# FFN1's down product by seven half-size products, and the modulation's rows made in three other places

## The chip, the cores and the metric

The kernel runs on one NeuronCore of a Trainium2 chip. The metric is the device time of one execution in microseconds, the median of several runs. Engines are called by their names: TensorE (PE), VectorE (DVE), ScalarE (ACT), GpSimd (POOL) and SyncE (SP), which issues nearly all transfers here.

## What is computed

One decoder layer in float32 on 1024 tokens of width 1024: a half step of a gated feed-forward network (FFN1), a mixer of two attention branches, and another half step (FFN2). Each is wrapped in norms, and nine rows of 1024 numbers, made from a conditioning vector c, shift, scale and gate them. Cut to what matters here:

```python
def swiglu(h, w_gate, w_up, w_down):
    return (jax.nn.silu(h @ w_gate) * (h @ w_up)) @ w_down          # 1024 -> 2816 -> 1024

mod = (jax.nn.silu(c) @ w_mod[l] + b_mod[l]).reshape(B, N_MOD, D_MODEL)
sh1, sc1, gt1, sh2, sc2, gt2, sh3, sc3, gt3 = [mod[:, j, None, :] for j in range(N_MOD)]
h = rms_norm(x, g_pre_ffn1[l]) * (1 + sc1) + sh1
x = x + 0.5 * gt1 * rms_norm(swiglu(h, w_gate1[l], w_up1[l], w_down1[l]), g_post_ffn1[l])
u = rms_norm(x, g_pre_mix[l]) * (1 + sc2) + sh2
y = hybrid_mixer(u, ...)      # branch A: sparse attention; branch B: three groups of dilated attention
x = x + gt2 * rms_norm(y, g_post_mix[l])
h = rms_norm(x, g_pre_ffn2[l]) * (1 + sc3) + sh3
x = x + 0.5 * gt3 * rms_norm(swiglu(h, w_gate2[l], w_up2[l], w_down2[l]), g_post_ffn2[l])
```

## The kernel before

Each matrix product in float32 is made of three matmuls on a high and a low part of both operands (`mm3`, lines 104 to 106); `split` (L76 on ACT, L77 on VectorE) makes the parts. The program is written stage by stage; a scheduler then puts each engine's instructions into one fixed order, and each engine works through its list in that order. A transfer is an entry of SP's list: while it waits for its buffer, all later transfers wait behind it.

The stages, in order of time:

- FFN1's gate and up (`gate_up`, 25 to 500 us): products by a scheme of seven half-size products instead of eight, 11 blocks `b` of 256 columns. The activations go to DRAM (`act1`).
- FFN1's down (`down`, 500 to 757 us): 22 slices of 128 rows of the weights by 8 token tiles and two halves of the columns, plainly, 352 matmuls on each line of `mm3`.
- The mixer: its first products (`cpj`), the indexer's scores, the top-k selection on VectorE (`topk`, 1035 to 1281 us) with the gates' products under it, branch B (`branch_b`: three groups of eight tiles, T0 to T23; tile T ends with the sum `ob`, L1064, and its store `bd<-ob`, L1069), branch A (`branch_a`, from 1445 us: keys `kpj` from the latents `gbuf`, scores `as`, and so on), and the output projection `wo`.
- FFN2: gate and up by `gate_up`, and down by `down7`, which is a scheme of seven half-size products as well, 308 matmuls on each line. It reads eight prepared operands per block from DRAM, which FFN2's `gate_up` writes with one more addition and two subtractions on POOL and one subtraction on VectorE (`operands`, lines 298 to 325, the subtractions on L302).

Rows 2 to 8 of the modulation come from `mod_rest`, a generator: one step loads a 128x512 piece of w_mod (`wr`, 256 KB), and VectorE multiplies it by a column of silu(c) and adds it to a sum (`macc`, L185; the first of eight by L183). After eight steps the sum over the partitions is made by two matmuls with a matrix of ones (`mo`), and half a row is stored. FFN1's gate_up and down call it as a filler, two steps at a time, in four buffers:

```python
r = pool.tile([P, 512], F32, name="wr", tag="wr", bufs=4)
nc.sync.dma_start(r, i["w_mod"][0, k * P:(k + 1) * P, c0:c0 + 512])
```

In `wo`, most norms (`residual`, `prenorm` and within them `rsqrt`, lines 84 to 100) are on POOL. Branch A's queries (`queries`, L1158) read 512-byte pieces from DRAM.

Of the kernel before, what the change touches and what calls it, by code (L numbers as in the profile page):

```python
# [10 lines left out]
F32 = mybir.dt.float32  # L11
# [12 lines left out]
P = 128  # L24
# [4 lines left out]
LATE = 2  # L29
FILL = 2  # L30
# [9 lines left out]
class Layer:  # L40
# [125 lines left out]
    def mod_rest(self, pool, rows):  # L166
# [3 lines left out]
        for v in (2, 3, 4, 5, 6, 7, 8):  # L170
            for h in range(2):
                c0 = v * D + h * 512
                acc = pool.tile([P, 512], F32, name="macc")
                for k in range(8):
                    r = pool.tile([P, 512], F32, name="wr", tag="wr", bufs=4)
# [12 lines left out]
                ah = pool.tile([P, 512], F32R, name="mah", tag="wr", bufs=4)  # L188
                al = pool.tile([P, 512], F32R, name="mal", tag="wr", bufs=4)
# [62 lines left out]
    def gate_up(self, W, raws, pools, V, wg, wu, actd=None, ad=None):  # L252
# [93 lines left out]
        def steps(order, filler=None, ahead=()):  # L346
# [4 lines left out]
            for s, (b, i) in enumerate(order):  # L351
# [4 lines left out]
                for m in range(2):  # L356
# [19 lines left out]
                    if i in (1, 4, 5, 6):  # L376
                        if m == 0:
                            nc.scalar.activation(x[0], x[0], AF.Silu)  # L378
                        else:
                            nc.gpsimd.tensor_tensor(x[1], x[1], x[0], op=ALU.mult)  # L380
                            if ad is not None:
                                operands(b, i, x)
                                continue
                            ff, h = {1: (0, 0), 4: (1, 0), 5: (1, 1), 6: (0, 1)}[i]
                            nc.sync.dma_start(actd[2 * b + ff, :, h * 512:(h + 1) * 512], x[1])
                if filler is not None and b >= len(early):
                    for _ in range(FILL):
                        next(filler, None)
# [11 lines left out]
    def down(self, W, wd, room, actd, y, G, junk, ss, post, filler=None):  # L400

        nc = self.nc
        NF = DFF // P
        tags = ("tr", "tr", "o", "gg", "pj", "pj", "s", "pt")
        got = [0]
        bg = iter(())
        for dh, tiles in ((0, range(8)), (1, range(4)), (1, range(4, 8))):
            bk = {t: self.bank("dn", tag=tags[t]) for t in tiles}
            halves = sorted({t // 4 for t in tiles})
            late, last = [], dh == 1  # L410
            nlate = LATE if dh and tiles[-1] == 7 else 1

            def mul(t, c, w, a):
                ts = slice((t % 4) * P, (t % 4 + 1) * P)
                ah, al = a[t // 4]
# [1131 lines left out]
```

## Time and profile before

| | |
|---|---|
| median of three runs | 2488.96 us (2488.2 to 2491.31) |
| profiled execution | 2492.64 us |
| its span, first to last instruction | 2490.9 us |
| mean granted clock of TensorE | 0.971 |
| busy: TensorE, VectorE, ACT, POOL | 2333.2, 1664.0, 1091.1, 1002.8 us |
| moved by DMA | 327.55 MB, 132 GB/s |

The profile comes from one execution. Busy time is given by engine and by stretch; a wait is put down to the instruction or the transfer that released it; the chain of waits follows the last instruction back to what released it, step by step. Names stand as "written <- read". TensorE's clock is given as a share of full speed.

### The profile page before, as it was taken

Reading aid. Unit: us, or ns where it says so; the run is one execution under the profiler, and the core shown is the slowest. Engines: PE = TensorE matmul, PEld = TensorE weight load, DVE = VectorE, ACT = ScalarE, POOL = GpSimd, SP = SyncE. Lnnn points to the kernel's source line nnn. Section 1 sums busy time; section 2 is a strip of 40 time slices with the busy share of each in tenths; the row PEclk is TensorE's granted clock in tenths of the full one; section 3 lists DMA queues with packets and bytes.
Section 4 is the critical chain, followed back from the end, with each engine's and each line's share of the span. In section 5 each row is a group of like instructions: output and inputs, shape, how many; then the busy total and the mean of one; then the engine's idle time right before and its main releaser. Section 6 shows DMA issues by size and latency. Waiting matters only on the chain.

```text
span 2490.9 us, 33864 instructions
## 1 busy us (share of the span) xinstructions
PE 2333.2 (94%) x11211; PEld 1956.6 (79%) x11211; DVE 1664.0 (67%) x3236; ACT 1091.1 (44%) x2346; POOL 1002.8 (40%) x1122
## 2 busy tenths in 40 slices
PE   5799999989998999999989799889889999999997
PEld 4588877778887977888989688768667888887876
DVE  7865779753886135899973378864477656555786
ACT  5432223323454345677635567632453333233443
POOL 5675555400004433242244200300488756652533
PEclk9899999999999999999999899999989999999999
DMA  9334554671543233521422422143343333336755
GB/s 280 92 103 127 150 156 147 222 268 51 182 137 107 78 100 99 177 63 35 131 85 59 108 69 69 52 169 127 127 135 117 126 108 111 94 123 232 245 194 203
DMA packets 244171, 327.55 MB, mean 132 GB/s; under 512 B 24535, under 2 KB 145271, under 8 KB 243997
## 3 DMA queue, kind: packets, MB, share of 16 engines
q1 hardware_dynamic: 243356, 324.33, 40.8%
q8 instruction: 89, 1.46, 0.2%
q10 hardware_dynamic: 640, 1.07, 0.1%
q14 instruction: 86, 0.70, 0.1%
HBM read 252.07 MB, written 73.27 MB: 131 GB/s over the span
## 4 chain that ended last, share of the span: by engine, by line
PE 69%; DVE 14%; DMA 7%; issue 4%; POOL 4%; ACT 3%; SPq 0%; DVEq 0%; POOLq 0%; ACTq 0%
PE gu L105 9%; PE gu L104 9%; PE gu L106 9%; PE dn L106 4%; PE dn L105 4%; PE dn L104 4%; PE gpj L104 2%; DMA wr<-in_w_mod_dram 2%; PE gpj L105 2%; PE gpj L106 2%; PE bq L104 2%; PE bq L105 2%; PE bq L106 1%; DMA re<-in_w_down_dram 1%; DVE wl L77 1%
## 5 line engine op out<-in xcount | busy, mean ns | idle before, releaser
L104 PE MATMUL gu<-V,wh 128*128 128x512 f32 x1232 | 489.6, 398 | 17.2 <-ACT wh L76 9.3
L105 PE MATMUL gu<-V,wl 128*128 128x512 f32 x1232 | 488.9, 397 | 6.6 <-DVE wl L77 5.7
L106 PE MATMUL gu<-V,wh 128*128 128x512 f32 x1232 | 484.3, 396 | 4.5 <-DVE V L77 4.5
L77 DVE TENSOR_TENSOR wl<-rw,wh 128x512 fp32r<-128x512 f32 x232 | 218.2, 943 | 111.3 <-PE gu L105 80.1
L104 PEld LDWEIGHTS gu<-V,wh 128*128 128x128 f32 x1232 | 235.4, 191 | 71.5 <-ACT wh L76 9.8
L105 PEld LDWEIGHTS gu<-V,wl 128*128 128x128 f32 x1232 | 235.0, 191 | 62.0 <-DVE wl L77 10.4
L106 PEld LDWEIGHTS gu<-V,wh 128*128 128x128 f32 x1232 | 234.6, 191 | 57.2 <-DVE V L77 7.7
L105 PE MATMUL dn<-dh,al 128*128 128x512 f32 x660 | 256.9, 392 | 0.2 <-DVE al L77 0.2
L106 PE MATMUL dn<-dl,ah 128*128 128x512 f32 x660 | 255.2, 392 | 1.1 <-DVE dl L77 1.0
L104 PE MATMUL dn<-dh,ah 128*128 128x512 f32 x660 | 239.0, 392 | 9.1 <-DVE junk L197 6.4
L76 ACT CAST wh<-rw 128x512 fp32r<-128x512 f32 x232 | 139.9, 618 | 213.1 <-PE gu L106 127.7
L372 DVE TENSOR_TENSOR p<-gu,p 128x512 f32<-128x512 f32 x252 | 169.8, 681 | 67.0 <-PE gu L106 33.6
L380 POOL TENSOR_TENSOR p<-p 128x512 f32<-128x512 f32 x86 | 132.1, 1537 | 202.9 <-DVE p L372 73.1
L104 PEld LDWEIGHTS dn<-dh,ah 128*128 128x128 f32 x660 | 124.3, 189 | 35.9 <-DVE junk L197 6.8
L378 ACT ACTIVATE p<-p 128x512 f32<-128x512 f32 x86 | 54.4, 633 | 222.2 <-DVE p L372 173.1
L106 PEld LDWEIGHTS dn<-dl,ah 128*128 128x128 f32 x660 | 124.6, 189 | 28.4 <-DVE dl L77 2.7
L105 PEld LDWEIGHTS dn<-dh,al 128*128 128x128 f32 x660 | 124.5, 189 | 27.3 <-DVE al L77 1.3
L185 DVE SCALAR_TENSOR_TENSOR macc<-wr,scol,macc 128x512 f32<-128x512 f32 x98 | 94.3, 962 | 52.7 <-DMA wr<-in_w_mod_dram 52.0
L76 ACT CAST dh<-rd 128x512 fp32r<-128x512 f32 x110 | 67.9, 619 | 117.5 <-PE dn L105 75.6
L77 DVE TENSOR_TENSOR dl<-rd,dh 128x512 fp32r<-128x512 f32 x110 | 77.1, 704 | 52.2 <-ACT dh L76 48.9
L104 PE MATMUL gpj<-uh,gw 128*128 128x512 f32 x256 | 103.8, 406 | 7.5 <-ACT gt L910 7.3
L849 DVE TENSOR_SCALAR_CACHE_REDUCE mask<-isc,cand 128x384 bf16<-128x384 f32 (+1 forms) x124 | 108.7, 877 | 2.6
(479 smaller groups left out, 5610.7 us busy)
## 6 DMA issues: line engine op xcount, KB each, us to landing
act<-p SPq DMA_DIRECT2D x122, 256.0 KB
rd<-in_w_down_dram SPq DMA_DIRECT2D x58, 512.0 KB
wr<-in_w_mod_dram SPq DMA_DIRECT2D x112, 256.0 KB
rw<-in_w_gate_dram SPq DMA_DIRECT2D x44, 512.0 KB
rw<-in_w_up_dram SPq DMA_DIRECT2D x44, 512.0 KB
ra<-act SPq DMA_DIRECT2D x35, 512.0 KB
act<-act SPq DMA_DIRECT2D x44, 256.0 KB
re<-in_w_down_dram SPq DMA_DIRECT2D x20, 512.0 KB
```

Source lines behind the costliest of these rows:

```text
L76: self.nc.scalar.copy(hi, src)
L77: self.nc.vector.tensor_sub(lo, src, f(hi))
L104: mm(out, ah, bh, start=start, stop=False)
L105: mm(out, al, bh, start=False, stop=False)
L106: mm(out, ah, bl, start=False, stop=stop)
L185: nc.vector.scalar_tensor_tensor(acc, r, self.scol[:, k:k + 1], acc, op0=ALU.mult, op1=ALU.add)
L372: nc.vector.tensor_tensor(x[m], bk, y[m], op=ALU.add)
L378: nc.scalar.activation(x[0], x[0], AF.Silu)
L380: nc.gpsimd.tensor_tensor(x[1], x[1], x[0], op=ALU.mult)
L849: nc.vector.tensor_scalar(mask[:, :(t + 1) * P], sc[t], 0.0 if v is None else one(f(v), t), 0.0, op0=op, op1=ALU.add, accum_out=one(cnt, t))
```

## The change

- FFN1's down is done by `down7` (now `down`, for both FFNs), and `down` of before is gone; FFN1's `gate_up` writes the eight operands.
- `mod_rest` is called for rows 2, 3, 4 in gate_up (one step at a time, the rest before down), for row 8 in down, and for rows 5, 6, 7 in branch B's last group, seven steps behind each tile, in memory of the indexer's scores (`isc3` is the sum, `isc4` and `isc5` the two load buffers, `isc6` the high part, `isc7` the row).
- All of `wo`'s norms are on VectorE, and a part of its weights has another place.
- The queries are stored in another layout, so that they are read in 4096-byte pieces and written in 512-byte ones.
- Branch B has three buffers for `ob` instead of two, and two for its weights instead of three.

```diff
-    def mod_rest(self, pool, rows):
+    def mod_rest(self, tile_, rows, vs):
...
-                acc = pool.tile([P, 512], F32, name="macc")
+                acc = tile_("macc", F32)
...
-                    r = pool.tile([P, 512], F32, name="wr", tag="wr", bufs=4)
+                    r = tile_("wr", F32)
...
-                ah = pool.tile([P, 512], F32R, name="mah", tag="wr", bufs=4)
-                al = pool.tile([P, 512], F32R, name="mal", tag="wr", bufs=4)
+                ah, al = tile_("mah", F32R), tile_("mal", F32R)
...
-                            if ad is not None:
-                                operands(b, i, x)
-                                continue
-                            ff, h = {1: (0, 0), 4: (1, 0), 5: (1, 1), 6: (0, 1)}[i]
-                            nc.sync.dma_start(actd[2 * b + ff, :, h * 512:(h + 1) * 512], x[1])
-                if filler is not None and b >= len(early):
-                    for _ in range(FILL):
-                        next(filler, None)
+                            operands(b, i, x)
+                if filler is not None:
+                    next(filler, None)
...
-    def down7(self, Ws, raws, wd, T, ad, y, G, junk, ss, post, nlate):
+    def down(self, Ws, raws, wd, T, ad, y, G, junk, ss, post, nlate, filler=None):
...
+                elif filler is not None:
+                    next(filler, None)
...
-            nc.sync.dma_start(self.qd[0, t], f(qh))
-            nc.sync.dma_start(self.qd[1, t], f(ql))
+            for l, x in enumerate((qh, ql)):
+                nc.sync.dma_start(self.qd[l, :, :, t, :].rearrange("e p q -> p e q"), f(x))
...
-    def branch_b(self, uT, W, bp, last, gates, raws):
+    def branch_b(self, uT, W, bp, last, gates, raws, mods):
...
                     last()
+                    self.mo, fill = "gg", mods()
...
-                ob = bp.tile([P, 264], F32, name="ob", bufs=2)
+                ob = bp.tile([P, 264], F32, name="ob", bufs=3)
...
+                for _ in range(7 if g == 2 else 0):
+                    next(fill, None)
+        for _ in fill:
+            pass
...
-                    nc.sync.dma_start(f(QQ[:, e, l]), self.qd[l, :, :, 2 * p + e, :].rearrange("t p q -> p t q"))
+                    nc.sync.dma_start(f(QQ[:, e, l]), self.qd[l, 2 * p + e])
...
+            mod = lambda vs: L.mod_rest(lambda name, dt: wk.tile([P, 512], dt, name=name, **(
+                {} if name == "macc" else dict(tag="wr", bufs=4))), jkf, vs)
+            fill = mod((2, 3, 4))
...
-            L.down(W, aps["w_down1"], room, actd, y, A1, lambda: jkb, ss, post1, fill)
+            L.down(Ws, raws, aps["w_down1"], lambda j: TT[j // 8][:, j % 8], ad, y, A1, lambda: jkb, ss, post1, 2, mod((8,)))
...
-        with pool("wb", 24) as W, pool("bp") as bp, pool("r3", 3) as L.rawp:
+        with pool("wb", 24) as W, pool("bp") as bp, pool("r3", 2) as L.rawp:
...
+            def mods():
+
+                place = lambda t, dt=F32: ixp.tile([P, (t + 1) * P], dt, name=f"isc{t}")
+                rows = place(7)
+                turns = cycle((4, 5))
+                at = lambda name: {"macc": 3, "mah": 6}.get(name) or next(turns)
+                return L.mod_rest(lambda name, dt: place(at(name), dt)[:, :512], [rows[:, :512], rows[:, 512:]], (5, 6, 7))
+
+            L.branch_b(uT, W, bp, lambda: L.topk(sc, ixp, mask, off, bp), lambda: L.gates(uT, gp), raws, mods)
...
-                    L.residual(ys[h][:, j, :], xt[:, j, :], ss[t], ss[t][:, 2:3], nc.vector if t in (4, 6) else nc.gpsimd)
+                    L.residual(ys[h][:, j, :], xt[:, j, :], ss[t], ss[t][:, 2:3], nc.vector)
                     nc.sync.dma_start(x2[tok(t), :], xt[:, j, :])
-                    L.prenorm(ys[h][:, j, :], xt[:, j, :], None, ss[t][:, 2:3], ss[t][:, 3:4], nc.vector if t in (5, 7) else nc.gpsimd)
+                    L.prenorm(ys[h][:, j, :], xt[:, j, :], None, ss[t][:, 2:3], ss[t][:, 3:4], nc.vector)
```

The order of VectorE in branch B's last group, before: around the sum of tile T20 (`ob_13273` is T21's, `ob_13393` T22's; `bP` are the softmax steps on scores `bs`, `bPT` the low parts of the transposed weights).

```order
L77 TENSOR_TENSOR bPT_13298<-bpt_13292,bPT_13297 128x512
L1037 ISA bP_13391,ob_13393<-bs_13394,res_6996 128x128
L1037 ISA ob_13393 128x1
L1037 ISA bP_13391,ob_13393<-bs_13394,res_6996 128x128
L1037 ISA ob_13393 128x1
L1037 ISA bP_13392,ob_13393<-bs_13401,res_6996 128x128
L1037 ISA ob_13393 128x1
L1037 ISA bP_13392,ob_13393<-bs_13401,res_6996 128x128
L1037 ISA ob_13393 128x1
L77 TENSOR_TENSOR bPT_13307<-bpt_13301,bPT_13306 128x512
L1064 TENSOR_TENSOR ob_13273<-bo_13310,ob_13273 128x256
L77 TENSOR_TENSOR bPT_13418<-bpt_13412,bPT_13417 128x512
```

The change, in the same group. The number behind `isc4` and `isc5` tells one load from the next, and the brackets name what an instruction waits for (DMAHW: a transfer).

```order
L978 ISA bP_13189,ob_13190<-bs_13198,res_6902 128x128 [waits PE_49]
L978 ISA ob_13190 128x1
L978 ISA bP_13189,ob_13190<-bs_13198,res_6902 128x128
L978 ISA ob_13190 128x1
L183 SCALAR_TENSOR_TENSOR isc3_13123<-isc5_13233,scol_99,isc3_13123 128x512 [waits DMAHW6_49,DVE_49]
L978 ISA bP_13313,ob_13315<-bs_13316,res_6902 128x256 [waits DMAHW7_49,PE_49]
L978 ISA ob_13315 128x1
L978 ISA bP_13313,ob_13315<-bs_13316,res_6902 128x256
L978 ISA ob_13315 128x1
L183 SCALAR_TENSOR_TENSOR isc3_13123<-isc4_13236,scol_99,isc3_13123 128x512 [waits DMAHW1_49,DVE_49]
L978 ISA bP_13314,ob_13315<-bs_13323,res_6902 128x256 [waits PE_49]
L978 ISA ob_13315 128x1
```

A modulation step that waits for its load now stands between the two softmax pairs and in front of the next ones.

SP's list, before: the load of branch A's latents, `gbuf`, stands among those of branch B's first position tables (`bcs`), and branch B's weights (`wbr`), with most of branch B's stores still to come.

```order
L944 DMA wbr<-in_w_in_dram 128x2x256 x3
L977 DMA bcs<-csd 128x96 x3
L1103 DMA gbuf<-ckvd 128x8x512
L977 DMA bcs<-csd 128x96 x2
L1069 DMA bd<-ob 128x264
L977 DMA bcs<-csd 128x96
```

The change: the same load (L1048 now) behind the last modulation loads, each of which waits for VectorE, and behind the store of the last tile's `ob`, a stored row and `br`, which reads branch B's results.

```order
L174 DMA isc5_13654<-in_w_mod_dram 128x512 [waits DMAHW7_49,DMAHW4_49,DVE_49]
L174 DMA isc4_13659<-in_w_mod_dram 128x512 [waits DMAHW2_49,DVE_49]
L174 DMA isc5_13662<-in_w_mod_dram 128x512 [waits DMAHW4_49,DVE_49]
L174 DMA isc4_13665<-in_w_mod_dram 128x512 [waits DMAHW5_49,DVE_49]
L1010 DMA bd_8353<-ob_13597 128x264 [waits DVE_49]
L1021 DMA br_15052<-bd_8353 128x792 [waits DMAHW1_49]
L197 DMA rows_76<-isc7_12567 1x512 [waits DVE_49]
L1021 DMA br_15147<-bd_8353 128x792 [waits DMAHW3_49]
L1048 DMA gbuf_13686<-ckvd_6386 128x8x512 [waits DMAHW6_49,DMAHW2_49,DMAHW7_49,PE_49,Activation_49]
```

`gbuf` moved from ahead of branch B's last two groups to behind them and the modulation, and waits for TensorE and ACT, which use its memory until then.

TensorE's list at the seam from branch B to branch A, before: the first key products and scores stand among branch B's last transposes (`bpt`) and value products (`bo`).

```order
L1056 MATMUL bo<-bV,bPT 128x128
L1059 MATMUL bo<-bV,bPT 128x64
L1048 MATMUL bpt<-ident,bP 128x128
L104 MATMUL kpj<-gbuf,wk 128x512
L105 MATMUL kpj<-gbuf,wk 128x512
L106 MATMUL kpj<-gbuf,wk 128x512
L104 MATMUL kpj<-gbuf,wk 128x512
L105 MATMUL kpj<-gbuf,wk 128x512
L106 MATMUL kpj<-gbuf,wk 128x512
L1048 MATMUL bpt<-ident,bP 128x128 x3
L104 MATMUL as<-KK,aq 128x512
L105 MATMUL as<-KK,aq 128x512
```

The change:

```order
L997 MATMUL bo<-bV,bPT 128x128 x2
L1000 MATMUL bo<-bV,bPT 128x64 x2
L188 MATMUL mo<-isc_13669,ones 128x512
L189 MATMUL mo<-isc_13670,ones 128x512
L102 MATMUL kpj<-gbuf,wk 128x512
L103 MATMUL kpj<-gbuf,wk 128x512
L104 MATMUL kpj<-gbuf,wk 128x512
L102 MATMUL kpj<-gbuf,wk 128x512
L103 MATMUL kpj<-gbuf,wk 128x512
L104 MATMUL kpj<-gbuf,wk 128x512
L102 MATMUL as<-KK,aq 128x512
L103 MATMUL as<-KK,aq 128x512
```

All of branch B and the last pair of modulation matmuls (`mo`) now stand ahead of the first `kpj`.

## Rows read from the trace of the kernel before

**Rows 1.** Windows: busy us of each engine (instructions), then TensorE clock, DMA share, GB/s.
```profile
24.00:500.00 476.00, 450.89 (x1934) 362.43 (x1935) 363.25 (x459) 157.72 (x280) 280.31 (x191) 0.97 0.50 152
501.00:757.00 256.00, 248.90 (x1096) 204.28 (x1094) 166.61 (x317) 107.74 (x202) 4.16 (x5) 0.98 0.46 151
...
1245.00:1282.00 37.00, 29.95 (x135) 28.25 (x135) 36.75 (x44) 8.98 (x20) 18.48 (x15) 0.90 0.27 78
1383.00:1452.00 69.00, 51.67 (x296) 46.14 (x295) 24.41 (x78) 33.50 (x96) 12.21 (x14) 0.78 0.39 95
2261.00:2476.00 215.00, 211.16 (x924) 172.59 (x922) 150.47 (x204) 93.26 (x181) 90.20 (x96) 1.00 0.67 229
```

**Rows 2.** PE groups by line, 500 to 757 us: xcount | busy us, mean ns | idle before.
```profile
L105 PE MATMUL dn<-dh,al 128*128 128x512 f32 x352 | 138.5, 393 | 0.2 <-DVE al L77 0.2
...
L122 PE MATMUL tr<-ident,y 128*128 128x128 f32 x32 | 4.6, 272 | 0.0
```

**Rows 3.** PE groups by line, 2260 to 2476 us.
```profile
L105 PE MATMUL dn<-dh,al 128*128 128x512 f32 x308 | 118.3, 390 | 0.0
```

**Rows 4.** Waits of PE, 495 to 870 us: us in total, times, longest.
```profile
PE dn L104 <- DVE junk L197: 6.4, 1, 6.4
PE cpj L104 <- ACT wc0h L81: 4.0, 1, 4.0
```

**Rows 5.** Line L302, what FFN2's gate/up adds for its operands: ns min/median/max.
```profile
L302 POOL TENSOR_TENSOR p<-p,p x22: 1287/1628/1804, 1908.7 to 2265.5; 128x512 f32<-128x512 f32 x22
L302 DVE TENSOR_TENSOR p<-p,p x11: 692/1784/1785, 1907.6 to 2263.6; 128x512 f32<-128x512 f32 x11
```

**Rows 6.** Chain of waits, 750 to 765 us: start us, us, what.
```profile
757.63 5.10 DMA wc0r<-in_w_in_dram
```

**Rows 7.** Tile wr, the modulation's loads and DVE steps over the whole span.
```profile
L185 DVE SCALAR_TENSOR_TENSOR macc<-wr,scol,macc x98: 731/751/1884, 230.2 to 685.1; 128x512 f32<-128x512 f32 x98
...
  DMA wr<-in_w_mod_dram: 75.9, 51
```

**Rows 8.** Chain of waits, 400 to 500 us, its pieces on wr loads.
```profile
433.64 2.92 DMA wr<-in_w_mod_dram
...
450.23 4.04 DMA wr<-in_w_mod_dram
...
464.99 2.57 DMA wr<-in_w_mod_dram
...
476.02 4.56 DMA wr<-in_w_mod_dram
```

**Rows 9.** SP timeline, 1383 to 1455 us: start us, us, line, DMA.
```profile
1383.13 0.32 SPq L1069 DMA_DIRECT2D bd<-ob  x1
...
1390.03 9.32 SPq L1158 DMA_DIRECT2D aq<-qd  x4
...
1403.04 0.86 SPq L1069 DMA_DIRECT2D bd<-ob  x2
...
1452.14 0.32 SPq L1069 DMA_DIRECT2D bd<-ob  x1
```

**Rows 10.** SP timeline, 1276 to 1300 us: branch A's latents are issued.
```profile
1282.63 0.37 SPq L1103 DMA_DIRECT2D gbuf<-ckvd  x1
```

**Rows 11.** DMA, 1281 to 1292 us, in 40 slices of 0.275 us.
```profile
GB/s 0 0 106 71 1 0 0 0 0 15 104 186 74 209 298 305 320 283 194 328 365 372 410 372 410 410 402 417 387 432 439 380 303 140 97 83 40 45 34 11
```

**Rows 12.** PE timeline, 1438 to 1447 us: branch A's first key and score products.
```profile
1441.63 0.80 PE L104 MATMUL kpj<-gbuf,wk 128*128 128x512 f32 x1
...
1445.23 0.64 PE L104 MATMUL as<-KK,aq 128*128 128x512 f32 x1
```

**Rows 13.** Line L94, a norm's small operation on either engine: ns min/median/max.
```profile
L94 DVE TENSOR_SCALAR rs_t<-rs_y,rs_v x63: 253/266/274, 697.6 to 2485.2; 128x1 f32<-128x1 f32 x63
L94 POOL TENSOR_SCALAR rs_t<-rs_y,rs_v x57: 334/341/1820, 1751.5 to 2482.9; 128x1 f32<-128x1 f32 x57
```

**Rows 14.** Waits of PE, 1760 to 1890 us.
```profile
PE tr L208 <- DVE wy L1302: 5.5, 4, 2.3
```

More of the change, by code (lines that the diff above doesn't have):

```diff
@@ L623, in rope, with load_w @@
         nc.vector.tensor_tensor(out2, out2, t[1], op=ALU.add)
-    def load_w(self, W, src, n, name, rows=1024, per=None, split=None, rawp=None):
+    def load_w(self, W, src, n, name, rows=1024, per=None, split=None, rawp=None, hi=None):
         nc = self.nc
-        per = per or 1024 // n
+        per, room = per or 1024 // n, hi
         his, los = [], []
@@ L635, in load_w @@
             for j in range(m):
-                hi = W.tile([P, n], F32R, name=f"{name}h", tag="w")
+                hi = W.tile([P, n], F32R, name=f"{name}h", tag="w") if room is None else room[:, k0 + j]
                 lo = W.tile([P, n], F32R, name=f"{name}l", tag="w")
@@ L1316, in layer_kernel @@
     sums = lambda: [L.const.tile([P, 4], F32, name="sums", bufs=8) for t in range(8)]
-    def rooms(fp):
-        r = [L.big.tile([P, 8, 512], F32, name="act", tag="big") for _ in range(4)]
-        f2 = [[fp[h].tile([P, 512], F32, name=f"act{c}{h}") for h in range(2)] for c in range(16, DFF // P)]
-        return [[r[2 * h + c // 8][:, c % 8] for h in range(2)] for c in range(16)] + f2
+    operands = lambda n: L.dram.tile([8, NB, P, 512], F32, name=f"act{n}")
     L.turns = gu_turns()
@@ L1328, in layer_kernel @@
     bigv = lambda i: L.big.tile([P, 2, 4, 512], F32R, name=f"V{i}", tag="big")
-    actd = L.dram.tile([DFF // P, P, S], F32, name="act1")
+    ad = operands(1)
     with pool("w1", 12) as W, pool("g1") as wk, pool("r1", 5) as L.rawp:
@@ L1378, in layer_kernel @@
         p1.close()
-        with pool("f1a") as fa, pool("f1b") as fp:
+        with pool("dr", 4) as dr, pool("dw", 14) as dw, pool("f1") as fp:
+            for _ in fill:
+                pass
             right.close()
             y1 = right.enter_context(pool("fy2", side="right")).tile([P, 4, D], F32, name="y1")
-            room = rooms((fa, fp))
-            y = [fa.tile([P, 4, D], F32, name="y0"), y1]
+            y = [L.big.tile([P, 4, D], F32, name="y0", tag="big"), y1]
+            TT = [L.big.tile([P, 8, 512], F32, name="TT", tag="big") for _ in range(2)]
             A1 = fp.tile([P, D], F32, name="A1")
@@ L1419, in layer_kernel @@
         L.turns = {}
[L1420 removed]
+        with pool("wa", 16) as W, pool("r2", 4) as L.rawp, pool("cp") as cp, pool("ce") as ce, pool("tb") as tb:
             def second():
@@ L1441, in layer_kernel @@
     x2 = L.dram.tile([S, D], F32, name="x2")
-    ad = L.dram.tile([8, NB, P, 512], F32, name="act2")
+    ad = operands(2)
     L.turns = {"pj": cycle(("pj", "s", "pj", "pt"))}
@@ L1463, in layer_kernel @@
                     cl = slice(c * 512, (c + 1) * 512)
-                    wh, wl = L.load_w(W, aps["w_o"][0][:, cl], 512, "wo")
+                    room = zp.tile([P, 8, 512], F32R, name="wohi", tag="z", bufs=3) if h and c else None
+                    wh, wl = L.load_w(W, aps["w_o"][0][:, cl], 512, "wo", hi=room)
                     for j in range(4):
```

77 lines of the change are left out of this document (12 added, 65 removed).

## The prediction

> **What bounds the kernel now.** I read the table of windows first, stage by stage [rows 1]. The FFN stages belong to TensorE: it is busy 248.9 of 256.0 us in FFN1's down product and 211.2 of 215.0 in FFN2's, at a granted clock near 1.0; in FFN1's gate/up the missing share is mostly the start. Two stretches do not belong to it. From 1245 to 1282 VectorE works 36.75 of 37 us (the end of the top-k selection) while TensorE has 29.95. From 1383 to 1452 (the last third of branch B) no engine is full: TensorE 51.7, VectorE 24.4, DMA share 0.39, clock 0.78; that stage is a chain of latencies. So matmuls taken from an FFN count in full, and a wait put into branch B's last third counts in full too. The change does both.
>
> **FFN1's down product: 30 us less (36 to 24).** Before, each of its three lines issues 352 matmuls [rows 2]; FFN2's scheme issues 308 [rows 3]. 132 matmuls go, at 211.16/924 = 0.229 us each [rows 1]: 30.2 us. The two windows differ by 41.0 us; of that the 32 transposes of the normed output, 4.6 us [rows 2], stay with FFN1, so 36 is the most. For the least I let the 3.8 us that FFN2's stage idles come more than twice, since FFN1's output also goes through VectorE's norms: 24. The 6.4 us that TensorE waits at the seam for VectorE's modulation row [rows 4] is part of the 36, not of the 30; the weights' and operands' first loads must still follow the last gate/up writes. DMA ran at 0.67 of its engines in FFN2's stage [rows 1], so the extra reads fit.
>
> **Its activations: 0 (3 either way).** gate/up now writes eight operands per block. That adds an addition and two subtractions on POOL, 1.63 us for a subtraction, and one subtraction on VectorE at 1.78 [rows 5], eleven times: 54 and 20 us. In 476 us POOL had 280 busy and VectorE 363, with three of the modulation's seven rows left of those that shared this stage and the next, and TensorE hides both. Four more writes of 256 KB per block, 11.5 MB, add 24 GB/s to 152. If that cover fails, POOL would need 476 busy us, and it stands at 334.
>
> **Start of the mixer: 5.5 us less (7 to 4).** TensorE waits 4.0 us for the first input weights [rows 4], issued at 757.63, after the last product, and 5.1 us under way [rows 6]. Now those loads are issued inside the last products. The 4.0 go, and I add 1.5 for the slow matmuls behind that idle time, an estimate.
>
> **End of top-k: 9 us more (5 to 18).** The order puts the first eight steps of modulation rows 5 to 7, and the ninth's start, between the last selection steps. Eight at 0.75 [rows 7] are 6 us of work on the engine that is full there; the least I allow is 5. Alone with their loads, nine at (3.2 + 0.75)/2 (below) would be 18. I take the work plus a third of the waiting; branch B's eighth tile, whose rotation stands later among these steps now, goes back with it. A third output buffer for branch B and one weight buffer less for it I cost at nothing, as the weights are loaded under the gates' matmuls; without that cover they are in the same 18.
>
> **Branch B's last third and the way into branch A: 42 us more (22 to 63).** The order puts the other 39 steps on VectorE between the output sums of tile 16 and tile 23, and gives their loads two buffers. A load can't be issued before the step two places back has read its buffer, and VectorE's queue stands still until it lands. In FFN1, with four buffers and under a full TensorE, VectorE already waited 75.9 us in 51 waits for such loads [rows 7], which cost nothing there. On the chain one such load takes 2.6 to 4.6 us [rows 8]; I take 3.2, below their mean of 3.5, as DMA is at 0.39 here and was at 0.50 there. A buffer turns in 3.2 + 0.75 us and there are two. The five ends of a half-row also use a buffer for the low part of the sum: 44 turns x 3.95/2 = 87 us, and one more us at each end for cast, subtraction and the matmul pair: 92. The 24 us of VectorE work that belong to branch B lie inside those waits. Before, the stores of tiles 16 and 23 were issued 69.0 us apart [rows 9], 9 of them behind SP's queue for the queries (1390.03, 9.32 us), which the new read order removes and which I therefore don't count again.
> The Trainium skill's page "DMA: Bandwidth & Descriptors", section "Anatomy of one DMA", fits a transfer as 2.0 us plus bytes over 436 GB/s; an estimate from it is 2.6 us for 256 KB. The trace agrees for the quickest piece on the chain, 2.57, and not for the slowest, 4.56; by the page alone the 87 would be 74 and the sum 13 less.
> Then the seam. Before, branch A's latents were loaded long ahead: issued at 1282.63 [rows 10], landed about 8 us later [rows 11]; the first scores began at 1445.23 [rows 12], 62.1 us after tile 16's store and before tile 23's. Now the latents lie in the memory that the modulation uses, so the order has them behind its last matmul. After the last step come about 2 us of cast, subtraction and matmuls, 8 of load, six key products at 0.43 at the slow clock (2.6) and 1.3 of splitting: 15. Tile 16 to first scores is 92 + 15 = 107 against 62; 3 us of branch B's own matmuls no longer lie among the scores: +42. Ends: 44 turns at 2.6 with no other cost and 13 at the seam, 74 + 13 - 62 - 3 = 22; at 3.9 with 18 there and 5 for the ends, 102 + 5 + 18 - 62 = 63.
>
> **Output projection: 4 us less (6 less to 3 more).** A small norm operation takes 266 ns on VectorE and 341 on POOL [rows 13], and TensorE waited 5.5 us for normed tiles [rows 14]. I take most of those; the other end is VectorE late with TensorE's transposed tiles, for which the same norms are now queued.
>
> **Sum.** -30 + 0 - 5.5 + 9 + 42 - 4 = +11.5, against the profiled execution's 2492.64 us (span 2490.9 plus 1.7): 2504. The median of the runs, 2488.96, is 3.7 below that execution, so I give 2500. All low ends together are -25 and all high ends +59.
>
> **Rivals.**
> *The loads hide (chance 0.22, faster).* Mechanism: in branch B's last third VectorE has 45 idle us of 69 and TensorE 17 [rows 1]; if loads go out early enough to land while VectorE waits for TensorE and ACT anyway, 39 steps x 0.75 = 29 us fill idle time and tile 23 comes no later. It decides on whether a load takes less than about 2.4 us more often than not (two buffers, 69 us for 44 turns: 3.1 a turn pair, less 0.75). Only the seam stays, 15 - 3 = 12 instead of 42, and 6 at the top-k: -30 - 5.5 + 6 + 12 - 4 = -21.5, that is 2467. Against it: no load on the chain was under 2.57. "Double-buffer for performance: Overlap DMA with compute" is a rule of the Trainium skill's page "Trainium Kernel Development and Optimization", section "Best Practices"; by that rule this rival would hold, and [rows 8] speak against it, as a load outlasts its step by more than three times.
> *FFN1's down is held up by data (chance 0.13, slower still).* Its reads share the queue on SP with gate/up's last writes and residual tiles; if it keeps 18 of the 30 us by stalls, the sum is +29.5: 2518. For it: DMA share stands at 0.67 with half the load of writes; against it: FFN2's same stage idles 3.8 us.
> *VectorE's order costs more than the ring (chance 0.10, slower still).* A score or sum of branch B queued behind a waiting step delays TensorE, which delays the next, so waits add instead of overlapping: the high end, 63 for 42: 2521.
> That the products don't shrink is excluded: the order has 616 dn matmuls on each line in all, where 660 stood.
>
> **Numbers.** The forecast has 0.55. A measurement of this kernel tells about 0.2%, 5 us, from no change: faster is below 2484, slower above 2494. Of the forecast's 0.55 I give 0.11 to within and 0.06 to faster, since its low ends reach 2464; of the first rival's 0.22, 0.19 to faster and 0.02 within; the two others are slower. Faster 0.25, within 0.13, slower 0.62. The range 2468 to 2530 takes in the first rival's time but for its own low side, the other two, and most of the unknown load times.
>
> **What would show it.** Right: 924 matmuls of FFN1's down in about 226 us; no wait of the mixer's first product for weights; in branch B's last third VectorE waiting for modulation loads, tile 16's store to tile 23's about 92 us, TensorE's clock there below 0.78; latents issued behind that, and first scores about 107 us after tile 16's store. Wrong: those stores 70 us apart or less; latents loaded early; FFN1's down above 235 us; or VectorE's modulation steps ended by branch B's data instead of loads.

## The result, and the profile after

The changed kernel takes 2530.94 us (median of four runs, 2528.42 to 2537.53) beside 2488.58 for the kernel before: a ratio of 1.0168, with a 95% interval of 1.015 to 1.0187. It is slower, as forecast, by 42 us and not by 11.5, and just outside the range, which ended at 2530. Its profiled execution took 2537.53 us (span 2535.7, mean granted clock 0.959).

Where the time went is read from the first instruction of each stage. In the views of single tiles, these three lines of the changed kernel tell when FFN1's down (`dn`), the mixer (`cpj`) and branch A's scores (`as`) begin: count, shortest, median and longest in ns, then first and last start.

```profile
L102 PE MATMUL dn<-dh,ah x616: 387/389/628, 515.8 to 2520.7; 128*128 128x512 f32 x154
...
L102 PE MATMUL cpj<-wc0h,uh x64: 331/334/689, 745.9 to 809.1; 128*128 128x384 f32 x64
...
L102 PE MATMUL as<-KK,aq x48: 221/396/792, 1504.8 to 1630.0; 128*128 128x512 f32 x24, 128*128 128x384 f32 x8, 128*128 128x128 f32 x8, 128*128 128x256 f32 x8
```

With tile 16's sum `ob`, tile 23's and the projection's first matmul from the same kind of view, the two profiles stand side by side (us; a stage of the same code differs by up to 5 us from one profile to the next, as gate/up of the kernel before shows below, and each stage is read from one profile of each kernel):

| from, to | before | after | difference | forecast |
|---|---|---|---|---|
| start to FFN1's down | 500.2 | 515.8 | +15.6 | 0 |
| down to the mixer's first product | 260.4 | 230.1 | -30.3 | -35.5 |
| that to tile 16's sum | 622.1 | 640.5 | +18.4 | +9 |
| tile 16's sum to the first scores | 62.5 | 118.4 | +55.9 | +45 |
| scores to the projection | 260.8 | 258.3 | -2.5 | -3 |
| projection to the last matmul of FFN2's down | 769.2 | 757.6 | -11.6 | -4 |
| sum | 2475.2 | 2520.7 | +45.5 | +11.5 |

The windows of the changed kernel answer to [rows 1] (columns as there): gate/up, a part of it, FFN1's down, the end of top-k, and branch B from tile 16 to 23.

```profile
24.00:516.00 492.00, 451.66 (x1929) 362.38 (x1930) 371.28 (x457) 159.61 (x280) 329.41 (x223) 0.97 0.51 156
200.00:300.00 100.00, 89.27 (x368) 71.23 (x366) 72.73 (x92) 25.35 (x45) 62.85 (x42) 0.95 0.57 177
516.00:746.00 230.00, 220.91 (x961) 178.61 (x961) 177.97 (x215) 106.75 (x204) 121.11 (x130) 0.99 0.67 227
1239.50:1305.80 66.30, 59.40 (x290) 56.52 (x288) 49.92 (x66) 20.46 (x49) 31.45 (x24) 0.95 0.36 109
1386.00:1486.00 100.00, 62.17 (x291) 52.78 (x290) 56.83 (x123) 34.03 (x93) 14.61 (x16) 0.63 0.58 164
```

FFN1's down has the looks of FFN2's in [rows 1], 961 matmuls with the transposes in 230 us, but VectorE is 178 us busy in it, where it was 167 of 256. And that is without a single modulation step, although `down` calls row 8's: the scheduler put all steps of FFN1, 64 of them, into gate/up.

```profile
L183 DVE SCALAR_TENSOR_TENSOR macc<-wr,scol,macc x56: 729/752/1847, 238.0 to 467.4; 128x512 f32<-128x512 f32 x56
L181 DVE TENSOR_SCALAR macc<-wr,scol x8: 486/933/1560, 234.1 to 452.7; 128x512 f32<-128x512 f32 x8
```

The kernel before has 75 of its 112 steps in gate/up and 37 in down. In gate/up of the changed kernel TensorE has 89 of 100 us between 200 and 300; it had 99.7 there before. In branch B's last third its clock fell to 0.63 (0.78 before).

### The profile page after: what moved, and what is told of

The parts are those of the page before. It is cut to its first block, busy times and chain, and to the rows that moved or that the text cites. A ratio compares the mean times of both kernels' runs of the same rounds, so it can differ in the third digit from the quotient of the medians.

```text
span 2535.7 us, 33916 instructions
## 1 busy us (share of the span) xinstructions
PE 2321.2 (92%) x11079; PEld 1939.5 (76%) x11079; DVE 1750.7 (69%) x3279; ACT 1092.8 (43%) x2350; POOL 1131.2 (45%) x1199
## 5 line engine op out<-in xcount | busy, mean ns | idle before, releaser
L75 DVE TENSOR_TENSOR wl<-rw,wh 128x512 fp32r<-128x512 f32 x232 | 233.3, 1009 | 116.7 <-PE gu L103 76.5
L103 PE MATMUL dn<-dh,al 128*128 128x512 f32 x616 | 239.4, 393 | 0.0
L104 PE MATMUL dn<-dl,ah 128*128 128x512 f32 x616 | 234.8, 395 | 3.0 <-DVE dl L75 2.9
L377 POOL TENSOR_TENSOR p<-p 128x512 f32<-128x512 f32 x86 | 132.2, 1539 | 156.4 <-DVE p L369 106.2
L75 DVE TENSOR_TENSOR al<-ra,ah 128x512 fp32r<-128x512 f32 x154 | 135.0, 889 | 32.6 <-ACT ah L74 25.1
L102 PEld LDWEIGHTS dn<-dh,ah 128*128 128x128 f32 x616 | 116.3, 189 | 30.8 <-ACT dh L74 6.1
L104 PEld LDWEIGHTS dn<-dl,ah 128*128 128x128 f32 x616 | 116.5, 189 | 29.7 <-DVE dl L75 5.4
L103 PEld LDWEIGHTS dn<-dh,al 128*128 128x128 f32 x616 | 116.3, 189 | 25.9 <-DVE al L75 0.2
L74 ACT CAST ah<-ra 128x512 fp32r<-128x512 f32 x154 | 93.0, 618 | 89.4 <-DMA ra<-act 48.6
L80 POOL TENSOR_TENSOR gw<-gr,gw 128x128 fp32r<-128x128 f32 x128 | 61.8, 494 | 110.0 <-ACT gw L79 106.1
L80 POOL TENSOR_TENSOR wl<-re,wh 128x512 fp32r<-128x512 f32 x16 | 23.6, 1490 | 194.5 <-ACT wh L79 186.6
```

What stands on the lines that cost most here:

```text
L74: self.nc.scalar.copy(hi, src)
L75: self.nc.vector.tensor_sub(lo, src, f(hi))
L80: self.nc.gpsimd.tensor_tensor(lo, src, f(hi), op=ALU.subtract)
L102: mm(out, ah, bh, start=start, stop=False)
L103: mm(out, al, bh, start=False, stop=False)
L104: mm(out, ah, bl, start=False, stop=stop)
```

## The experiments

Theory one, behind the prediction: the modulation costs time wherever its loads aren't covered, above all in branch B, where two buffers and a load's own time set the pace. Rivals: the operands make gate/up long; the place counts, not the number of loads; the small parts move more than the large ones.

**Gate/up: the pace of the filler.** In gate/up of the changed kernel, these waits of TensorE (us in total, times, longest) had grown, the first, on sums of the modulation whose loads came late, from nothing, the second from 2.8:

```profile
PE mo L188 <- ACT mah L74: 9.3, 3, 5.1
...
PE gu L102 <- DVE p L369: 8.1, 5, 2.9
```

So the first experiment gave the filler its old pace:

```diff
-                if filler is not None:
-                    next(filler, None)
+                if filler is not None and b >= len(early):
+                    for _ in range(2):
+                        next(filler, None)
```

> The changed kernel, but FFN1's gate/up calls the modulation's filler as before (from the sixth block on, two steps at a time) instead of one step at a time from the first. Theory: the 15.6 us that gate/up became longer are TensorE's waits for sums whose loads come late, since the first pairs of sum matmuls stand early in its list: then FFN1's down begins near 501 to 505 us instead of 515.8, and the total falls by 11 to 15 us, to 2516 to 2520. Rival: they are the price of the eight operands (POOL, VectorE, four more writes per block): then down still begins at 512 to 516 and the total stays within 4 us of 2531.

Measured: 2533.02 us, and down begins at 515.0. The theory missed. The wait on sums is gone from the list, and others stand in its place:

```profile
PE gu L103 <- DVE wl L75: 9.8, 12, 1.8
...
PE gu L102 <- DVE p L369: 5.4, 6, 3.0
```

VectorE's low parts of the weights (`wl`) are late now. It was not the place of the sums alone.

**Gate/up without the modulation.** The next one takes the filler out of gate/up; rows 2 to 4 are called behind it.

```diff
-            GU([...] + [(b, i) for b in range(EARLY, NB) for i in range(7)], fill)
+            GU([...] + [(b, i) for b in range(EARLY, NB) for i in range(7)])
```

> The changed kernel without the modulation's filler in FFN1's gate/up: rows 2 to 4 are all made between gate/up and down, where the scheduler finds room. Theory now: operands and modulation fit into gate/up each alone (before had the second, FFN2 has the first, both with a TensorE that hardly waits) and not together; then TensorE's waits from 200 us to gate/up's end fall from 17 us to 4 or less, and gate/up's last matmul comes at 500 to 505 us; the rows then cost some time ahead of down, so the total moves by -15 to +10. Rival: the operands alone are too much for gate/up; it still ends at 511 or later.

Measured: 2572.71 us. Down begins at 494.9, earlier than in any profile of the changed kernel and no later than in the kernels with FFN1 as before (500.2 before, 495.7 and 495.8 in two runs below). The windows 300 to 400, and behind gate/up, and TensorE's largest wait from 495 to 780:

```profile
300.00:400.00 100.00, 100.00 (x437) 81.72 (x436) 54.78 (x69) 31.70 (x53) 71.53 (x49) 1.00 0.34 109
495.00:560.00 65.00, 41.74 (x155) 29.99 (x153) 48.30 (x60) 19.58 (x35) 30.68 (x20) 0.78 1.02 366
```

```profile
PE mo L188 <- ACT mah L74: 28.6, 3, 17.3
```

The scheduler still takes 16 of the 64 steps into gate/up, all before 290 us; from 200 to 300 TensorE has 97.9 of 100 us. From 300 on there are operands and no modulation, and TensorE is full, 100 of 100 us. The kernel before has modulation and no operands there, and 98.3. Each alone fits, both together do not, as the expectation said: 48 steps more make the start of down 20.9 us later (515.8). Whether VectorE's time for them or their loads' share of the DMA does it, the runs do not separate. The total was underrated: 48 steps behind gate/up, where operands and weights of the down product load at a DMA share of 1.02, stop TensorE for 28.6 us at three pairs of sum matmuls; down to mixer takes 285.6 us instead of 230.1.

**All of the modulation as before.** Rows 2 to 8 by the old filler in FFN1 (two steps at a time, in gate/up from the sixth block on), none in branch B:

```diff
-            fill = mod((2, 3, 4))
+            fill = mod((2, 3, 4, 5, 6, 7, 8))
...
-            L.down(Ws, raws, ..., post1, 2, mod((8,)))
+            L.down(Ws, raws, ..., post1, 2, fill)
...
-                    self.mo, fill = "gg", mods()
...
-                for _ in range(7 if g == 2 else 0):
-                    next(fill, None)
```

> The changed kernel with all seven modulation rows made in FFN1's gate/up and down, at the old pace, and none in branch B. Theory: modulation in branch B costs the way from tile 16's store to branch A's first scores 56 us over before, and the end of top-k some 10 to 18: that way is then 58 to 66 us again (117.9 now), the latents are loaded early, gate/up ends near 501, and the total is 2440 to 2465. Rival 1: the operands make gate/up long, and it still ends at 512 to 516: 2455 to 2480. Rival 2: VectorE is full in the down product with 28 modulation steps beside the sums, and down takes 240 us or more instead of 230: 2450 to 2475 with gate/up at 501.

Measured: 2498.56 us, ratio 1.0044 to before (1.0021 to 1.0068). Branch B does what the theory said, and better: 50.1 us from tile 16's sum to the first scores, latents issued at 1309. Yet the total is 34 to 59 us above what was expected. Down begins at 523.1, later than rival 1's 512 to 516, and takes 264.8 us to the mixer's first product: more than the plain product of before. It has 32 steps in it (not the 28 that were expected). Rival 2 has the time right, and not its reason: VectorE is 203 of 265 us busy, not full. TensorE's waits from 500 to 800 us:

```profile
PE dn L102 <- ACT dh L74: 7.1, 3, 3.8
PE mo L188 <- ACT mah L74: 5.9, 2, 4.0
PE dn L104 <- DVE dl L75: 5.4, 5, 1.5
PE dn L103 <- DVE al L75: 5.1, 4, 2.1
```

Every one of them is for a part that VectorE or ACT makes, or for a sum. The 30 us that the stage gained in the changed kernel are those of a down product without modulation.

**One row in branch B.** Row 5 alone there, three steps behind each tile; rows 6 and 7 with row 8 in FFN1's down:

```diff
-            L.down(Ws, raws, ..., post1, 2, mod((8,)))
+            L.down(Ws, raws, ..., post1, 2, mod((8, 6, 7)))
...
-                return L.mod_rest(..., (5, 6, 7))
+                return L.mod_rest(..., (5,))
...
-                for _ in range(7 if g == 2 else 0):
+                for _ in range(3 if g == 2 else 0):
```

(In `down` the filler is emptied behind the fifth product.)

> The changed kernel with only row 5 made in branch B (three steps behind each tile), rows 6 and 7 beside row 8 in FFN1's down. Theory (the time goes by the number of loads through two buffers): tile 16's store to tile 23's falls from 99.6 us to 69 to 78, the seam behind it stays at 15 to 19 us if the latents still wait for the last step, and the total falls by 20 to 35 us unless down gets longer. Rival (it goes by the place, whatever the number: queries, keys and the seam in one queue): those stores stay 90 us apart or more and the total falls by less than 12.

Measured: 2487.55 us, ratio 0.9982 to before (0.9969 to 0.9994), and 43 us less than the changed kernel, where 20 to 35 were expected. Tile 16's to tile 23's sum takes 61.5 us (69 to 78 were expected, and 57.8 is what it takes with no row at all). The number of loads counts, the rival falls. The 32 steps of rows 6 and 7 in FFN1's down (from 532 to 682 us) cost 14 us there: 244.1 us from down to mixer. In the run with the modulation as before, 32 steps in the same stage (523 to 653 us) cost 34.7, so their number alone does not set the price.

**One buffer for the loads.** Four buffers have no room in the memory of the scores (of its places only `isc3` to `isc7` are wide enough, and all five are used), so the other direction was tried:

```diff
-                turns = cycle((4, 5))
...
-                at = lambda name: {"macc": 3, "mah": 6}.get(name) or next(turns)
+                at = lambda name: {"macc": 3, "mah": 6, "mal": 5, "wr": 4}[name]
```

> The changed kernel with one buffer instead of two for branch B's modulation loads (the other holds only the low part of a finished sum). Theory (a load's own time over the number of buffers sets the pace): the 39 steps from tile 16's sum to the last step take about (3.2 + 0.75) us each, some 150 to 175 us instead of 99.7 to tile 23's sum or shortly after it, the first scores come 165 to 195 us after tile 16's sum (118.4), and the total rises by 50 to 80 us. Rival (the pace is set by the order of VectorE's list or by the bytes that DMA moves, and the buffers hardly matter): first scores within 15 us of 118, total up by less than 20.

Measured: 2559.3 us, 28 more than the changed kernel; the first scores come 142.5 us after tile 16's sum. Between the two expectations: the scheduler put eight steps more ahead of tile 16, and 31 loads were left for this stretch instead of 39. The first line of these loads in SP's timeline, the longest run without others between, and the last:

```profile
1385.47 0.36 SPq L174 DMA_DIRECT2D isc<-in_w_mod_dram  x1
...
1466.70 17.75 SPq L174 DMA_DIRECT2D isc<-in_w_mod_dram  x6
...
1505.56 0.33 SPq L174 DMA_DIRECT2D isc<-in_w_mod_dram  x1
```

From 1385.47 to 1505.56 are 30 turns, 4.0 us each: the 3.2 + 0.75 us of the prediction. Six in a row come at 3.5. So the mean turn was sized rightly, and with one buffer it is the pace; the mean also holds the ends of half-rows. VectorE's wait for these loads from 1380 to 1540:

```profile
DVE isc L183 <- DMA isc<-in_w_mod_dram: 52.7, 26, 6.0
```

**Another queue for the loads.**

```diff
-                    nc.sync.dma_start(r, i["w_mod"][0, k * P:(k + 1) * P, c0:c0 + 512])
+                    nc.scalar.dma_start(r, i["w_mod"][0, k * P:(k + 1) * P, c0:c0 + 512])
```

> The changed kernel with the modulation's loads issued by ACT instead of SP, in all places, the same buffers. Theory (in branch B a load's own time and two buffers set the pace): tile 16's store to tile 23's stays at 92 to 102 us (99.7), and gate/up ends no earlier than 512. Rival (SP's list is what is late: loads stand behind stores that wait for POOL, and behind keys and queries): that stretch falls to 85 us or less and gate/up ends at 500 to 508; the total falls by 20 to 30.

Measured: 2525.14 us. Tile 16 to 23 takes 96.5 us, down begins at 509.9. The rival (SP's list) falls for branch B; for gate/up the 6 us are hardly more than profiles differ. Two loads that ACT issues while queries and keys are under way, and the two steps that wait for them:

```profile
1404.23 0.33 ACTq L174 DMA_DIRECT2D isc<-in_w_mod_dram  x1
1406.94 0.33 ACTq L174 DMA_DIRECT2D isc<-in_w_mod_dram  x1
```

```profile
1413.67 0.75 DVE L183 SCALAR_TENSOR_TENSOR isc<-isc,scol,isc 128x512 f32<-128x512 f32 x1 [1.47 <-DMA isc<-in_w_mod_dram]
...
1416.33 0.75 DVE L183 SCALAR_TENSOR_TENSOR isc<-isc,scol,isc 128x512 f32<-128x512 f32 x1 [1.90 <-DMA isc<-in_w_mod_dram]
```

Loads are used in the order of their issue, so each of these took over 9 us to land, though ACT's queue has nothing but such loads there.

**Rows 5 to 7 before the top-k.** In the mixer's first products and the indexer's scores, where VectorE seemed to have room:

```diff
                 nc.scalar.copy(nat[:, t % 2, :], b[:, :nn])
+                for _ in range(2):
+                    next(fill, None)
...
             b4 = b[:, :256].rearrange("p (h x e) -> p h x e", h=8, x=2)
+            for _ in range(3):
+                next(fill, None)
```

> The changed kernel with rows 5 to 7 made in the mixer's first products and the indexer's scores (three load buffers, one raw buffer less there) instead of in branch B. Theory: that stage is TensorE's, VectorE is 42 to 55% busy in it, so 48 steps and their waits are covered there: tile 16 to the first scores goes from 118 to 50 to 62 us, the end of top-k gets back some 8, and the total is 2455 to 2475, less than both kernels. Rival: VectorE leads to the top-k there, and its start comes 20 us or more later behind the first mixer product than the 279 us now: total 2480 to 2495.

Measured: 2496.85 us, ratio 1.0029 (1.0017 to 1.0041). The kernel was run once more for its profile:

> The kernel of the run with rows 5 to 7 before the top-k once more, for its profile: that run's total was 2497 us, some 30 above what the theory said. If VectorE leads there, the way from the mixer's first product to tile 16's sum is 660 to 675 us (640.5 in the changed kernel); if the down product is held up by row 8 or by late loads, the way from its first matmul to the mixer's first is 245 to 265 (230.1).

Measured: 2492.92 us. Branch B is as short as it gets, 48.3 us from tile 16's sum to the first scores; down to mixer takes 230.4. What was saved is lost between: 670.1 us from the mixer's first product to tile 16's sum, where it is 630.4 with no step in the mixer and in branch B (the run with the modulation as before). TensorE's waits from 740 to 1060, and the window 760 to 870:

```profile
PE mo L188 <- ACT mah L74: 9.5, 3, 7.1
PE ctr L638 <- DVE nat L633: 9.2, 3, 5.9
...
PE cpj L102 <- ACT cjunk L626: 5.1, 4, 1.7
```

```profile
760.00:870.00 110.00, 73.51 (x395) 64.32 (x394) 74.25 (x129) 32.84 (x90) 53.07 (x144) 0.83 0.53 165
```

TensorE has 73.5 of 110 us there, at a clock of 0.83. VectorE was not full (74 us). The sums, and the transposes that need VectorE's normed rows, wait in TensorE's list for VectorE, which stands 13.9 us for these loads in the window. The mean busy share of VectorE, on which the theory's "covered" rested, said nothing of that.

**The small parts.** The projection's norms back on POOL, in the changed kernel:

```diff
-                    L.residual(..., ss[t][:, 2:3], nc.vector)
+                    L.residual(..., ss[t][:, 2:3], nc.vector if t in (4, 6) else nc.gpsimd)
...
-                    L.prenorm(..., ss[t][:, 3:4], nc.vector)
+                    L.prenorm(..., ss[t][:, 3:4], nc.vector if t in (5, 7) else nc.gpsimd)
```

> The changed kernel with the output projection's norms on POOL and VectorE as before. Theory: the norms on VectorE are what made the way from the projection's first matmul to the end 11.6 us shorter, so it is 7 to 12 us longer here, the total 2538 to 2543. Rival: the weights' new place and the order did it, and the total moves by less than 4 us.

Measured: 2536.2 us, 5 more, between the two expectations; the way from the projection to the end is 763.4 us (757.6 with the norms on VectorE, 769.2 before). The 11.6 us lie in two stages. From the projection's first matmul to FFN2's gate/up it is 105.9 us before, 102.4 in the changed kernel and 106.8 here: that part is the norms'. From FFN2's gate/up to its down product it is 448.8, 440.9 and 440.3: 8 us that are not theirs. TensorE's waits on tiles that it transposes come to 10.5 us in this kernel, in three lines, and to 7.3 in the changed one, in two:

```profile
PE tr L205 <- DVE wy L1247: 4.5, 3, 2.4
PE tr L205 <- DVE wy L211: 3.8, 3, 2.7
PE tr L205 <- DVE rs_v L86: 2.2, 1, 2.2
```

```profile
PE tr L205 <- DVE wy L1247: 6.0, 2, 4.0
...
PE tr L205 <- ACT wy L213: 1.3, 3, 0.7
```

Branch B's weight buffers and output buffers as before (`ob` two, `r3` three):

> The changed kernel with branch B's weights in three buffers and its output in two, as before. Theory: with two, the gates' products (the work that fills TensorE between branch B's first tiles) are used up earlier, and TensorE lacks 8 us of work between 1120 and 1220 us: from the mixer's first product to tile 16's sum falls from 640.5 us to 628 to 636, the total by 4 to 10. Rival: the 18 us there come from the top-k's end alone, and the total stays within 3 us of 2531.

Measured: 2534.79 us, 640.4 us to tile 16's sum. Nothing of the 18.4 us there is theirs. From tile 16's sum to tile 23's it takes 105.9 us here and 99.7 in the changed kernel, which speaks for the third output buffer, by one profile of each.

Then, the kernel before with the queries' read order alone, and with that and the projection's part (norms and the place of its weights):

> The kernel before with the queries' read order alone. Theory: only the stall on SP's list goes (queries issued in 9.3 us, with branch B's stores behind), so tile 16's sum to the first scores goes from 62.5 to 50 to 56 us and the total falls by 6 to 12. Rival: the 512-byte writes that it moves to the queries' stage cost as much there, and the total stays within 3 us.

> The kernel before (plain down product, modulation as it was) with two of the change's small parts: the queries' read order, and the output projection's norms on VectorE with its weights' new place. Theory: these two parts gain by themselves; the way from tile 16's sum to the first scores goes from 62.5 to 50 to 56 us, from the projection to the end from 769 to 753 to 760, and the total is 2461 to 2473, less than both kernels. That puts the loss of the whole change on the seven products together with the modulation, at 55 us or more. Rival: the parts gain only in the changed kernel's order; total 2482 to 2492.

Measured: 2485.51 us with the queries alone (ratio 0.9998, 0.9986 to 1.0011), and 62.0 us from tile 16's sum to the scores: the stall of 9.32 us on SP's list [rows 9] cost nothing, and the gain that both theories put there did not come (64.9 us with both parts). With the projection's part 2470.99 us, ratio 0.994 (0.9919 to 0.9962): 15 us less than before and 60 less than the changed kernel, as that theory said for the total. Most of the gain is behind the projection's first matmul, 758.1 us to the end instead of 769.2: 102.3 to FFN2's gate/up and 441.2 from there to its down product, where the kernel with the queries alone has 106.2 and 448.9. So the 8 us go with the weights' new place; by what means is not shown.

**This is the version that beats both**: the kernel before, its FFN1 and its modulation untouched, with the projection's norms on VectorE, its weights' new place and the queries' read order, which alone gains nothing.

## Why the prediction was right in sign and wrong in size

Four terms of the sum came out worse than forecast and one better: gate/up by 15.6 us, FFN1's down with the mixer's start by 5, the end of top-k by 9, branch B with its seam by 11; the output projection gave 8 more than forecast. The sum missed by 34.

- **FFN1's down**: 30.3 us were gained, where -30 and -5.5 for the mixer's start were forecast. The 132 matmuls alone are 30.2 by the prediction's price. Of what is missing, 4.6 us are a wait of TensorE's transposes for one of the last normed tiles; 5.4 more of that kind come behind the mixer's first product, and so fall in the next row of the table. The stage also lost the 37 modulation steps that it had before: with 32 steps in it, it takes 244.1 or 264.8 us, so the products' own gain is not measured apart from that.
- **"Its activations: 0"** is the step that failed first. The text asked whether POOL is full (329 of 492 us, it is not) and took a TensorE that hides both; it counted on three rows there, and four came (64 steps, fewer than the 75 of before). The run without filler shows that operands are hidden (494.9), the kernel before that modulation alone is; the two together made gate/up 15.6 us longer. An engine that works through a fixed list is late before it is full: TensorE stopped at single places for a sum, a product (`p`) or a low part (`wl`).
- **End of top-k, +9**: 18.4 us were measured up to tile 16. Of these, 5.5 lie ahead of the selection (279.8 us from the mixer's first product, 274.3 before), where TensorE now has the wait of 5.4 us for normed tiles; they belong to the new down product. Top-k's counting under the gates' products is no longer than it was, but the stretch behind it, up to 1305.8, takes 66.3 us and not 50.3; VectorE has 50 us of work in it, with nine steps. The counting before, the stretch behind it before, then the counting in the changed kernel and with the modulation as before:

```profile
1034.90:1250.00 215.10, 212.25 (x1186) 191.03 (x1184) 202.68 (x642) 150.49 (x364) 72.45 (x104) 0.99 0.32 97
1250.00:1300.30 50.30, 43.26 (x212) 40.47 (x211) 38.44 (x53) 14.75 (x38) 21.04 (x18) 0.90 0.25 77
```

```profile
1025.70:1239.50 213.80, 199.25 (x1105) 174.48 (x1104) 198.22 (x639) 144.32 (x354) 63.66 (x97) 0.98 0.29 86
```

```profile
1067.80:1277.20 209.40, 198.76 (x1108) 175.20 (x1107) 198.31 (x639) 144.65 (x355) 64.08 (x98) 0.99 0.30 88
```

TensorE issues 81 matmuls fewer under the counting and 78 more behind it (290 for 212). It idles 2.9 us in the first window, and 14.6 and 10.6 in the two others: the gates' products, which fill it, come earlier in the order (last one at 1094.5 us; 1174.7 before). Branch B's buffers are not why; what moved them was not found. Without any step in branch B the same way takes 630.4 us, 8.3 more than before; so 10 of the 18.4 go with the nine steps (9 forecast). But they do not go by their number: the kernel with one load buffer has seventeen steps ahead of tile 16's sum, and 641.9 us.
- **Branch B's last third, 92 us**: 98.4 from tile 16's sum (1386.4) to the cast of the last modulation sum (1484.8), and 99.7 to tile 23's. Mechanism and turn were right (VectorE's waits below; the 75.9 of [rows 7] were more, but stood under a nearly full TensorE).

```profile
DVE isc L183 <- DMA isc<-in_w_mod_dram: 29.7, 28, 2.6
DVE isc L181 <- DMA isc<-in_w_mod_dram: 6.6, 4, 2.9
```

Missing in the sum was one burst of other loads. On the chain of waits most pieces are the 2.6 to 3.5 us that were expected, and one is 10.75, behind a piece of 10.15 on a load of branch B's own (`bV`):

```profile
1398.39 10.15 DMA bV<-vd
...
1408.62 10.75 DMA isc<-in_w_mod_dram
...
1420.24 2.71 DMA isc<-in_w_mod_dram
...
1423.82 2.83 DMA isc<-in_w_mod_dram
...
1427.53 3.43 DMA isc<-in_w_mod_dram
```

SP's timeline tells what it stood behind: queries (`aq`) and keys, 4 MB, which the order of before had in this stretch too:

```profile
1403.25 2.99 SPq L1103 DMA_DIRECT2D aq<-qd  x2
1407.28 0.58 SPq L1064 DMA_DIRECT2D Ke<-krd  x1
1407.91 0.61 SPq L1064 DMA_DIRECT2D Ko<-krd  x1
1408.62 0.54 SPq L174 DMA_DIRECT2D isc<-in_w_mod_dram  x1
```

The mean DMA share of 0.39, from which the load's time was chosen, hid that burst. It is not a matter of SP's queue alone: issued by ACT, loads of the same burst took over 9 us. The Trainium skill's page "DMA: Bandwidth & Descriptors", section "Anatomy of one DMA", from which 2.6 us was estimated, gives its fit for transfers that GpSimd issues, and these are SP's; the trace agrees with it for the quick loads (2.71 here, and 3.48 - 0.75 = 2.73 a turn in the six of the one-buffer run), and not for the one in the burst.
- **The seam, 15 us**: 20.0 from that cast to the first scores. From the issue of the latents to the first key product are 11 us and not 8: the product also needs the weights `wk`, whose load was issued behind the latents and ended TensorE's wait of 14.2 us.

The last tile's store, the latents, the first key product and the first scores, in the timeline (SP's and PE's lines):

```profile
1486.51 0.33 SPq L1010 DMA_DIRECT2D bd<-ob  x1
...
1490.18 0.37 SPq L1048 DMA_DIRECT2D gbuf<-ckvd  x1
...
1501.15 0.29 PEld L102 LDWEIGHTS kpj<-gbuf,wk 128*128 128x128 f32 x1 [14.66 <-ACT wk L74]
...
1504.78 0.28 PEld L102 LDWEIGHTS as<-KK,aq 128*128 128x128 f32 x1 [1.39 <-ACT KK L74]
```

- **Output projection, -4**: -11.6. The norms gave about 4, as said; the 8 us in FFN2's gate/up go with the weights' place, which the prediction did not price. Of the transposes' waits before, [rows 14] shows one line of three; together they are 13.4 us.
- The rival in which the loads hide falls with three rows, as VectorE waited 36 us for them, and nearly holds with one (61.5 us beside 57.8 with none). The rule of the Trainium skill's page "Trainium Kernel Development and Optimization", section "Best Practices", to double-buffer did not save it: two buffers overlapped seven steps in this stretch and not 39, though with one the first scores came 24 us later still. The rival of a down product held up by data falls. That of VectorE's list costing more than the ring is not shown: the burst is enough for the 6 us by which 98.4 exceeds 92.

Not settled: why the modulation as before leaves 50.1 us from tile 16's sum to the scores and the kernel before 62.5 (not the queries: 62.0 with them; the third output buffer may be part of it), what moved the gates' products forward, and whether four buffers in branch B would have hidden the loads, which was not tried for want of room.

## What to carry to other kernels

Work that rides along for nothing is paid by slack at single points of the lists, not by the mean busy share of its engine: before its host is made faster or gets other work, ask where it goes, and price it there with its loads. Here 112 small steps cost little in the old FFN1 (the one long wait of TensorE for them is the 6.4 us of [rows 4]) and more in every other place tried: 20.9 us for 48 in the new gate/up (515.8 beside 494.9), 39.7 for 48 in the mixer's first products (670.1 beside 630.4), 14.0 or 34.7 for 32 in the new down product, and 78.4 for 48 in branch B (68.3 behind tile 16's sum, 10.1 ahead of it). In every mix that was tried they came to more than the 30 us by which the down product became shorter. When several parts of a change come together, try the small ones on the old kernel: two of them on it beat both.

## What was not expected of the hardware

- Reads in pieces of 4096 bytes instead of 512 shortened the issue of the four query loads (9.32 us to 1.96), and the kernel by nothing measurable (2485.51 beside 2486.35 us).
- A 256-KB load behind 4 MB of other loads in the same queue took 10.75 us from issue to landing, beside 2.7 to 3.4 for its neighbours. Two loads in another queue took over 9 us during the same burst.
- Loads from ACT's queue instead of SP's changed the stretch from tile 16 to 23 by 3 us of 99.7, no more than profiles differ.
